# Output weights split once into stored hi and lo tiles, between attention and retention of a hybrid decoder step

## The chip, the cores and the metric

The kernel runs on one core of one Trainium2 chip. The metric is device time in microseconds (us). Engines are named as in the profile: PE multiplies matrices (PEld loads its weights), DVE is the vector engine, ACT the scalar engine, POOL the GpSimd engine, SP the engine that issues most DMAs. Matmul results land in PSUM, other tiles lie in SBUF, and "scratch" tensors lie in DRAM.

## The reference, cut to what matters

1024 prompt tokens and 64 decode tokens (8 sequences of 8) go through one decoder layer; T = 1088 tokens in all. The mixer has two halves, retention and windowed attention, and both are concatenated ahead of one output projection:

```python
    hn = rms_norm(x, norm_mix_gain)
    proj = hn @ w_in
    q_r, k_r, v_r, g_r, q_s, k_s, v_s = jnp.split(proj, cuts, axis=-1)
    ...
    o_r, new_ret = retention(q_r, k_r, v_r, ret_state, chunk)
    o_r = rms_norm(o_r).reshape(b, t, RET_WIDTH) * jax.nn.silu(g_r)
    ...
    o_s = swa_prompt(q_s, k_s, v_s, attn_sinks)       # decode tokens: swa_sample over a cached window
    ...
    h = x + jnp.concatenate([o_r, o_s], axis=-1) @ w_out
    hf = rms_norm(h, norm_ffn_gain)
    h = h + jnp.square(jax.nn.relu(hf @ w_up)) @ w_down
```

`w_out` is 1024 x 1024.

## The kernel before, in words

Every large product is made of three matmuls: each operand is split into a rounded part "hi" (a cast on ACT to `float32r`) and the rest "lo" (a subtraction on DVE or POOL), and `mm3` adds hi x hi, lo x hi and hi x lo.

The stages, in order of time: the projections for attention; attention over the prompt in eight blocks (`swa_block`), with the retention's q, k and gate projections running beside it (`psf`, `psg` are their PSUM tiles, `gst` the gate tiles); attention of the decode tokens; values and retention in blocks of 128 tokens; the output projection, for the first 544 tokens while retention still runs (`out_early`), then for the second 544 (`out_parts`); the squared-ReLU MLP, first up, then down, which takes the time from about 500 us on.

The code is written in program order and a list scheduler sets the order on each engine; that order is fixed in the built program, and each engine works through its own list. SP's list is a queue of DMA issues: one that waits holds up those behind it. A tile pool with `bufs=n` hands out n buffers for a tag in turn; a new tile waits for the last reader of the one that had its buffer.

Names at the place of the change:

- Prompt attention uses tag `s` (three buffers of 4 KB per partition, softmax scores) and tag `pt` (two buffers, transposed probabilities).
- Decode attention uses one more `s` tile, `s8`. Scores are matmuls `sc` in two rounds (the profile's `sc<-smp,q`); DVE turns each round into `s8` (L480, `s<-smp,nsl,sc`), takes maxima (L350 to L355), ACT the exponentials (L358, after loading its table), POOL multiplies by the inverse sums (L365), PE transposes (`pps`), DVE copies (`pt8`), PE multiplies with the values (`po8`), ACT and DVE split the result (`mhs`, `mls`), and SP stores both.
- Only then does SP load the first tiles of retention (`qt8`, `kt8`, L546 and L547), and PE begins retention of the decode tokens with `rsr8` (L633). Value block 1 is tied behind that by an explicit order (`queued`), and value blocks 8 and 0 (`pst`, weights `wv_hi`, `wv_lo`) come ahead of it.
- The output weights: `wo_pair` loads half rows of two weight tiles into `raw` (three buffers), and `wsplit` (L791, L792) makes hi and lo of each on ACT and DVE (tag `wa`, four buffers). Each weight is split for each half of the tokens, so there are 32 splits of 128 x 512. `mix_load(1, ...)` loads the attention rows of the second half of the tokens from DRAM (`mixah`, `mixal`).

The lines that tie the value blocks to decode retention (`next, decode` runs a step of it; `queued` issues behind the last matmul of what came before), and the split:

```python
    value_block(8)
    ins = value_block(0)
    ins = queued(ins, next, decode)
    ins = queued(ins, value_block, 1)
    ins = queued(ins, next, decode)
    ...
    def halve(hi, lo, src, lo_eng):
        nc.scalar.copy(hi, src)                                        # L791
        lo_eng.tensor_tensor(lo, src, hi.bitcast(F32), ALU.subtract)   # L792
```

Of the kernel before, what the change touches and what calls it, by code (L numbers as in the profile page):

```python
# [11 lines left out]
F32 = mybir.dt.float32  # L12
F32R = mybir.dt.float32r
AF = mybir.ActivationFunctionType
ALU = mybir.AluOpType
# [5 lines left out]
P = 128  # L21
# [8 lines left out]
def tok_tile(t):  # L30
    off = 960 if t == 8 else t * 128
    c = min(off // 384, 2)
    return off, c, off - CH[c][0]
# [3 lines left out]
def hymba_layer(ctx: ExitStack, tc: tile.TileContext, a: dict, o: dict):  # L37
    nc = tc.nc
# [10 lines left out]
    scratch = ctx.enter_context(tc.tile_pool(name="scratch", bufs=1, space=DRAM))  # L49

    def slot(i, dt, name):
        return slots.tile([P, 3072], dt, tag=f"s{i}", name=name)
# [13 lines left out]
    def wload(src, kk, name, lo_eng="p", parts=2, after=()):  # L66
        hi = ring.tile([P, 2048], F32R, tag="whi", name=name + "_hi")
        lo = ring.tile([P, 2048], F32R, tag="wlo", name=name + "_lo")
        n = 2048 // parts
        after = list(after)  # L70
        for h in range(2):
            raw = ring.tile([P, 1024], F32, tag="raw", name=f"{name}_raw{h}", bufs=3)
            for q in range(0, 1024, n):
                nc.sync.dma_start(raw[:, q : q + n], src[:, h * 1024 + q : h * 1024 + q + n])
                if after:
                    load_x(*after.pop(0))
            for q in range(0, 1024, n):
                h_, l_ = (v[:, h * 1024 + q : h * 1024 + q + n] for v in (hi, lo))
                r_ = raw[:, q : q + n]
                nc.scalar.copy(h_, r_)  # L80
                eng = nc.vector if lo_eng[(2 * h + q // n) % len(lo_eng)] == "v" else nc.gpsimd
                eng.tensor_tensor(l_, r_, h_.bitcast(F32), ALU.subtract)
        return hi.rearrange("p (k n) -> p k n", k=kk), lo.rearrange("p (k n) -> p k n", k=kk)
# [44 lines left out]
    g_d = scratch.tile([P, 4, T], F32, name="g_d")  # L128
    ms_hi_d = scratch.tile([P, 4, T], F32, name="ms_hi_d")
    ms_lo_d = scratch.tile([P, 4, T], F32, name="ms_lo_d")  # L130
    y_d = scratch.tile([P, 4, 4, 2, Q], F32, name="y_d")
    u_d = [scratch.tile([P, 2, 2, 7, Q], F32, name=f"u_d{g}") for g in range(8)]

# [87 lines left out]
    sp = attn.enter_context(tc.tile_pool(name="swa", bufs=2))  # L221
# [84 lines left out]
    w = wload(a["w_in"][2], 8, "wkv", "v")  # L306
    for t in range(9):
        off, c, r0 = tok_tile(t)
# [14 lines left out]
        pt = psB.tile([P, 512], F32, tag="t2", name="ptk")[:, :128]  # L323
# [112 lines left out]
            )  # L436


    pr = psB.tile([P, 512], F32, tag="t2", name="prq8")
    for t4 in range(4):  # L440
        col_sums(pr[:, t4 : t4 + 1], q8s[:, t4, :], ones[:, 0:1])
# [19 lines left out]
        nc.sync.dma_start(d_, a[s_])  # L461
    nc.sync.dma_start(o["kc"][:, :, 0:120], kc[:, :, 8:128])
    nc.sync.dma_start(o["vc"][0:120], vc[8:128])
    s8 = sp.tile([P, 4, 256], F32, tag="s", name="s8", bufs=3)[:, :, :192]
    for tt in range(2):
        ps = psB.tile([P, 512], F32, tag="t1", name="sc8")
        for t4 in (2 * tt, 2 * tt + 1):
# [18 lines left out]
    for h, n in ((0, 128), (1, 64)):  # L486
        pp = transposed(s8, h * 128, n, "s")
        pt = nt.tile([P, 512], F32, tag="ntmp", name=f"pt8{h}")
# [20 lines left out]
    for blk in range(4):  # L509
        w = wload(a["w_in"][3 + blk], 8, f"wqk{blk}")  # L510
        dst = qr_d if blk < 2 else kr_d
        for j in range(2):
            m = (blk % 2) * 2 + j
# [6 lines left out]
    for blk in range(2):  # L520
        w = wload(a["w_in"][7 + blk], 8, f"wg{blk}")
# [244 lines left out]
    def mix_block(t, mt, gt):  # L766
        off, c, r0 = tok_tile(t)
        d0 = 64 if t == 8 else 0
        pm = psB.tile([P, 512], F32, tag="t2", name="pm")
        for p_ in range(4):  # L770
            nc.tensor.transpose(
                pm[:, p_ * 128 + d0 : p_ * 128 + 128], mt[d0:, p_ * 128 : p_ * 128 + 128], ident[d0:, d0:]
            )
        src = pm.rearrange("p (k n) -> p k n", k=4)[:, :, d0:]
        g_ = gt[:, :, d0:]
        nc.vector.tensor_tensor(g_, src, g_, ALU.mult)
        for s in range(2):
            b0, b1 = max(off + d0, 2 * Q * s), min(off + 128, 2 * Q * s + 2 * Q)
            if b0 < b1:
                hi, lo = (mix[s, "r" + x].rearrange("p k h n -> p k (h n)")[:, :, b0 - 2 * Q * s : b1 - 2 * Q * s] for x in "hl")  # L780
                g1 = gt[:, :, b0 - off : b1 - off]
                nc.scalar.copy(hi, g1)
                nc.gpsimd.tensor_tensor(lo, g1, hi.bitcast(F32), ALU.subtract)


    def pool(name, bufs=1, side=None, space=None):
        kw = {"space": space} if space else {}
        return tc.tile_pool(name=name, bufs=bufs, side=side, reuse_waits="tile", **kw)
# [5 lines that stand above are left out]
    def wsplit(src, tag, name, lo_eng):  # L794
        w = (mid if tag == "wb" else mw).tile([P, 2, 512], F32R, tag=tag, name=name, bufs=4)
        halve(w[:, 0, :], w[:, 1, :], src, lo_eng)
        return w
# [14 lines left out]
    def mix_load(s, pl):  # L812
        for x, d_ in zip("hl", (ms_hi_d, ms_lo_d)):
            t_ = mix[s, "a" + x] = pl.tile([P, 4, 2, Q], F32R, tag="mixa" + x, name=f"mixa{x}{s}")
            nc.sync.dma_start(
                t_.bitcast(F32).rearrange("p k h n -> p k (h n)"), d_[:, :, 2 * Q * s : 2 * Q * s + 2 * Q]
            )

    def wo_pair(s, m, half):

        raw = mw.tile([P, 1024], F32, tag="raw", name=f"wo{half}{s}_{m}_raw", bufs=3)
        c0 = 512 * (half == "a")
        nc.sync.dma_start(
            raw.rearrange("p (m n) -> p m n", m=2), a["w_out"][m : m + 2, :, c0 : c0 + 512].rearrange("m p n -> p m n")
        )
        for i in range(2):
            yield wsplit(raw[:, i * 512 : i * 512 + 512], "wa", f"wo{half}{s}_{m + i}", nc.vector)

    def out_half(s, half, ps, h, w, first, last):
        for k in range(4):  # L830
# [29 lines left out]
    def out_parts(s, ms, half, psum, pss):  # L860

        for m in ms:
            if m % 2 == 0:
                gen = wo_pair(s, m, half)
            w = next(gen)
            for h in range(2):
                if half == "a":
                    pss[m, h] = psum()
                out_half(s, half, pss[m, h], h, w, half == "a", half == "r")
# [74 lines left out]
    qbh, qbl, kh, kl = split_space([ring.tile([P, 1024], F32R, tag="raw", name=f"qk{i}", bufs=3) for i in range(3)])  # L944
    for i, x in enumerate("hl"):
        mix[0, "r" + x] = slot(6 + i, F32R, "mixr" + x)[:, : 8 * Q].rearrange("p (k h n) -> p k h n", k=4, h=2)
    held, mxr, mxrx = {}, None, ExitStack()
    for t in range(5):
        if t == 0:
            for _ in range(2):  # L950
# [4 lines left out]
        if t == 1:  # L955
            hn0x.close()
            mxr = mxrx.enter_context(pool("mxr"))
# [10 lines left out]
    mw = ctx.enter_context(pool("mw", side="right"))  # L968
# [10 lines left out]
    def out_early(m):  # L979

        if m and m % 2 == 0:
            gens["a"], gens["r"] = (wo_pair(0, m, x) for x in "ar")
            ahead.extend(next(gens[x]) for x in "ar")
        wa_, wr_ = ahead
        ahead.clear()
        if m % 2 == 0:
            ahead.extend(next(gens[x]) for x in "ar")
        pss = [early() for h in range(2)]
        for h in range(2):
            out_half(0, "a", pss[h], h, wa_, True, False)  # L990
            out_half(0, "r", pss[h], h, wr_, False, True)
        residual(0, m, pss)()

    gens = {x: wo_pair(0, 0, x) for x in "ar"}
    ahead = [next(gens[x]) for x in "ar"]
    mix_block(4, *held[4])
    for t in (5, 6, 7):
        mt = retention_block(t)
        for m in (2 * t - 10, 2 * t - 9):
            out_early(m)  # L1000
        if t == 6:
            with tc.issue_after(last_load[0].ins):
                mix_load(1, mxA)
        mix_block(t, *mt)
# [218 lines left out]
    for g, (f0, nf) in enumerate(((0, 2), (2, 4), (6, 4), (10, 4), (14, 2))):  # L1223
# [7 lines left out]
        for i in DOWN:  # L1231
# [38 lines left out]
            n = 7 * g - 7 + DOWN.index(i)  # L1270
# [128 lines left out]
```

## Time and profile before

| | |
|---|---|
| median of three runs | 1189.5 us (1188.86 to 1191.59) |
| the profiled execution, whole time | 1188.43 us |
| its span | 1186.7 us |
| PE busy | 1169.6 us |
| DVE busy | 839.1 us |
| ACT busy | 513.8 us |
| POOL busy | 494.2 us |
| granted TensorE clock | 1.00 |

The span runs from the first to the last instruction of the program, and the time of the execution has 1.7 us around it. Busy time is an average over stages: which engine a stage waits for has to be read in that stage. A matmul's row lasts longer than PE is held by it (successive rows overlap), so the pitch of their starts is PE's pace.

### The profile page before, as it was taken

What the parts mean: (1) busy time and instruction counts of PE and PEld (TensorE: products, weight loads), DVE (VectorE), ACT (ScalarE), POOL (GpSimd) and SP (SyncE); (2) the same over time, 40 slices, a digit from 0 to 9 for tenths busy, and PEclk for the clock granted to TensorE, in tenths of its full rate; (3) what the DMA queues carried; (4) which work ended last, traced back from release to release, by engine and by line L of the source; (5) the groups of instructions that cost most, each with busy time, mean ns of one, the idle gap of its engine ahead of it and who ended that gap; (6) DMA issues with size and microseconds to landing.
All of it is one profiled execution on the core that took longest, in us unless ns stands there. A gap on an engine that the chain in (4) does not pass through costs nothing.

```text
span 1186.7 us, 23488 instructions
## 1 busy us (share of the span) xinstructions
PE 1169.6 (99%) x9405; PEld 1123.5 (95%) x9405; DVE 839.1 (71%) x1546; ACT 513.8 (43%) x1055; POOL 494.2 (42%) x393
## 2 busy tenths in 40 slices
PE   8999999999999999999999999999999999999998
PEld 7999988989778899999999999999989999999998
DVE  7556868632257769887766667666788787888676
ACT  8343544553334347644444444444642333333231
POOL 0125333332255542467666666566383142053000
PEclk9999999999999999999999999999999999999999
DMA  7221235333525555343444434444685456443225
GB/s 247 73 62 68 93 102 166 104 115 98 180 74 168 181 183 156 113 156 133 141 151 148 144 130 141 151 148 157 236 290 157 148 169 203 143 155 104 76 59 187
DMA packets 102277, 169.44 MB, mean 143 GB/s; under 512 B 12000, under 2 KB 68256, under 8 KB 101912
## 3 DMA queue, kind: packets, MB, share of 16 engines
q1 hardware_dynamic: 88807, 123.80, 31.5%
q10 hardware_dynamic: 10800, 35.23, 9.3%
q0 software_dynamic: 2560, 8.91, 2.3%
q8 instruction: 74, 1.21, 0.4%
q14 instruction: 36, 0.29, 0.1%
HBM read 114.30 MB, written 53.61 MB: 142 GB/s over the span
## 4 chain that ended last, share of the span: by engine, by line
PE 81%; DVE 6%; DMA 5%; issue 3%; ACT 2%; POOL 2%; SPq 0%; ACTq 0%; DVEq 0%; POOLq 0%
PE psd L176 9%; PE psd L177 9%; PE psd L175 9%; PE psx L175 5%; PE psx L177 5%; PE psx L176 5%; PE psz L175 2%; PE psz L177 2%; PE psz L176 2%; PE pst L175 2%; PE pst L176 2%; PE pst L177 2%; PE psf L175 2%; PE psf L177 2%; PE psf L176 2%
## 5 line engine op out<-in xcount | busy, mean ns | idle before, releaser
L175 PE MATMUL psd<-uh,wd_w 128*128 128x272 f32 x896 | 258.4, 288 | 3.2 <-DVE a L1267 2.4
L176 PE MATMUL psd<-uh,wd_w 128*128 128x272 f32 x896 | 259.3, 289 | 0.0
L177 PE MATMUL psd<-ul,wd_w 128*128 128x272 f32 x896 | 257.9, 288 | 0.7 <-DVE ul L792 0.7
L175 PEld LDWEIGHTS psd<-uh,wd_w 128*128 128x128 f32 x896 | 169.1, 189 | 4.3 <-DVE a L1267 3.4
L177 PEld LDWEIGHTS psd<-ul,wd_w 128*128 128x128 f32 x896 | 168.7, 188 | 0.9 <-DVE ul L792 0.9
L176 PEld LDWEIGHTS psd<-uh,wd_w 128*128 128x128 f32 x896 | 168.4, 188 | 0.0
L1267 DVE TENSOR_TENSOR a<-a,psd 128x272 f32<-128x272 f32 x248 | 101.9, 432 | 48.9 <-PE psd L177 48.8
L792 DVE TENSOR_TENSOR wu_w<-wu_s,wu_w 128x512 fp32r<-128x512 f32 x64 | 61.9, 971 | 49.8 <-ACT wu_w L791 49.2
L791 ACT CAST wd_w<-wd_s 128x512 fp32r<-128x512 f32 x64 | 37.5, 621 | 119.0 <-PE psd L177 107.2
L792 DVE TENSOR_TENSOR ul<-ur,uh 128x1088 fp32r<-128x1088 f32 x56 | 84.0, 1527 | 4.1 <-ACT uh L791 4.1
L1120 DVE SCALAR_TENSOR_TENSOR m<-m,rsf 128x272 f32<-128x272 f32 x96 | 72.9, 760 | 3.2 <-ACT rsf L914 0.5
L175 PE MATMUL psx<-op_1h,wu_w 128*128 128x272 f32 x256 | 74.3, 290 | 0.4 <-ACT m L1136 0.4
L177 PE MATMUL psx<-op_1l,wu_w 128*128 128x272 f32 x256 | 74.1, 289 | 0.0
L175 PE MATMUL psx<-op_0h,wu_w 128*128 128x272 f32 x256 | 74.1, 290 | 0.0
L177 PE MATMUL psx<-op_0l,wu_w 128*128 128x272 f32 x256 | 74.1, 289 | 0.0
L176 PE MATMUL psx<-op_1h,wu_w 128*128 128x272 f32 x256 | 73.7, 288 | 0.0
L176 PE MATMUL psx<-op_0h,wu_w 128*128 128x272 f32 x256 | 73.7, 288 | 0.0
L365 POOL TENSOR_TENSOR sp<-sp,ssp 128x1024 f32<-128x1024 f32 (+1 forms) x16 | 28.6, 1787 | 88.4 <-DVE ssp L364 60.1
L791 ACT CAST uh<-ur 128x1088 fp32r<-128x1088 f32 x56 | 59.7, 1101 | 12.7 <-PE psd L176 9.1
L175 PE MATMUL psf<-hnh,wqk_hi 128*128 128x384 f32 (+1 forms) x192 | 63.5, 331 | 0.2 <-DVE qkst L517 0.2
L177 PE MATMUL psf<-hnl,wqk_hi 128*128 128x384 f32 (+1 forms) x192 | 63.2, 329 | 0.0
L176 PE MATMUL psf<-hnh,wqk_lo 128*128 128x384 f32 (+1 forms) x192 | 62.8, 327 | 0.0
(343 smaller groups left out, 3619.4 us busy)
## 6 DMA issues: line engine op xcount, KB each, us to landing
ur<-u_d SPq DMA_DIRECT2D x53, 544.0 KB, 5.2
u_d<-r4t SPq DMA_DIRECT2D x32, 544.0 KB, 4.6
wu_r<-in_w_up ACTq DMA_DIRECT2D x32, 512.0 KB, 4.4
wd_r<-in_w_down ACTq DMA_DIRECT2D x30, 512.0 KB, 6.5
u_d<-r3t SPq DMA_DIRECT2D x32, 408.0 KB, 2.9
y<-in_xY POOLq DMA_DIRECT2D x16, 272.0 KB, 3.5
y_d<-y POOLq DMA_DIRECT2D x16, 272.0 KB, 3.2
yt<-y_d SPq DMA_DIRECT2D x16, 272.0 KB, 2.9
```

The lines of the kernel that those rows point to most:

```text
L175: nc.tensor.matmul(ps, lh, rh, start=first, stop=False, skip_group_check=more)
L176: nc.tensor.matmul(ps, ll, rh, start=False, stop=False, skip_group_check=more)
L177: return nc.tensor.matmul(ps, lh, rl, start=False, stop=last, skip_group_check=more)
L365: nc.gpsimd.tensor_tensor(s, s, ss.unsqueeze(2).broadcast_to([P, 4, n]), ALU.mult)
L791: nc.scalar.copy(hi, src)
L792: lo_eng.tensor_tensor(lo, src, hi.bitcast(F32), ALU.subtract)
L1120: nc.vector.scalar_tensor_tensor(t_, src, 0.0, rsf[:, s, h, :], ALU.max, ALU.mult)
L1267: added[i] = nc.vector.tensor_tensor(to, to, ps, ALU.add).ins
```

## The change

Between prompt attention and decode attention a new loop loads each of the eight weight tiles whole, splits both halves of it on ACT and DVE, and stores hi and lo side by side in DRAM (`wo_d`) by DMAs that POOL issues. It takes its raw tiles from tag `s` and its split tiles from tag `pt`. `s8` is asked for ahead of the loop. `wo_pair` then loads a split half tile (512 KB) straight into one of seven buffers, four of tag `wa` and three of tag `raw`, with no work on ACT or DVE. The second half's attention rows are loaded one retention block later (`t == 7`).

```diff
+    wo_d = [scratch.tile([P, 2, 1024], F32, name=f"wo_d{m}") for m in range(8)]
...
+    s8 = sp.tile([P, 4, 256], F32, tag="s", name="s8", bufs=3)[:, :, :192]
+    for m in range(8):
+        raw = sp.tile([P, 4, 256], F32, tag="s", name=f"wo_raw{m}", bufs=3).rearrange("p k n -> p (k n)")
+        nc.sync.dma_start(raw, a["w_out"][m])
+        for c in (slice(0, 512), slice(512, 1024)):
+            w = sp.tile([P, 2, 512], F32R, tag="pt", name=f"wo_hl{m}")
+            nc.scalar.copy(w[:, 0, :], raw[:, c])
+            nc.vector.tensor_tensor(w[:, 1, :], raw[:, c], w[:, 0, :].bitcast(F32), ALU.subtract)
+            nc.gpsimd.dma_start(wo_d[m][:, :, c], w.bitcast(F32))
+
     pr = psB.tile([P, 512], F32, tag="t2", name="prq8")
...
-    s8 = sp.tile([P, 4, 256], F32, tag="s", name="s8", bufs=3)[:, :, :192]
...
     def wo_pair(s, m, half):
-        raw = mw.tile([P, 1024], F32, tag="raw", name=f"wo{half}{s}_{m}_raw", bufs=3)
         c0 = 512 * (half == "a")
-        nc.sync.dma_start(
-            raw.rearrange("p (m n) -> p m n", m=2), a["w_out"][m : m + 2, :, c0 : c0 + 512].rearrange("m p n -> p m n")
-        )
         for i in range(2):
-            yield wsplit(raw[:, i * 512 : i * 512 + 512], "wa", f"wo{half}{s}_{m + i}", nc.vector)
+            tag, bufs = ("raw", 3) if len(w_loads) % 7 > 3 else ("wa", 4)
+            w = mw.tile([P, 2, 512], F32R, tag=tag, name=f"wo{half}{s}_{m + i}", bufs=bufs)
+            w_loads.append(nc.sync.dma_start(w.bitcast(F32), wo_d[m + i][:, :, c0 : c0 + 512]))
+            yield w
...
-        if t == 6:
+        if t == 7:
             with tc.issue_after(last_load[0].ins):
                 mix_load(1, mxA)
```

The line numbers of the kernel after are 10 higher from the loop on (L480 becomes L490, L633 becomes L643).

The first place is decode attention on DVE; the rows start where `s8`'s scale is ready. Before:

```order
L453 TENSOR_SCALAR nsl8_2162<-nsl8_2162,nslope_287 128x4 [waits DVE_49]
L480 SCALAR_TENSOR_TENSOR s8_2177<-smp_2171,nsl8_2162,sc8_2178 128x192 [waits DVE_49]
L480 SCALAR_TENSOR_TENSOR s8_2177<-smp_2171,nsl8_2162,sc8_2197 128x192
L526 TENSOR_TENSOR gst_3230<-psg_3205,rsb_177 128x384 [waits DMAHW7_49,PE_49]
L480 SCALAR_TENSOR_TENSOR s8_2177<-smp_2171,nsl8_2162,sc8_2178 128x192 [waits PE_49]
L480 SCALAR_TENSOR_TENSOR s8_2177<-smp_2171,nsl8_2162,sc8_2197 128x192 [waits PE_49]
```

After, the rows that end the same way (`wo_hl5` is the split of weight 5, its two rows the halves a and b; DMASW is a DMA issued by POOL, here the store of the half two earlier):

```order
L447 TENSOR_TENSOR wo_hl4_2179<-wo_raw4_2177,wo_hl4_2179 128x512 [waits DMASW6_49,DMAHW4_49,DVE_49,Activation_49]
L447 TENSOR_TENSOR wo_hl4_2183<-wo_raw4_2177,wo_hl4_2183 128x512 [waits DMASW7_49,Activation_49]
L447 TENSOR_TENSOR wo_hl5_2189<-wo_raw5_2187,wo_hl5_2189 128x512 [waits DMAHW6_49,DMASW0_49,Activation_49]
L447 TENSOR_TENSOR wo_hl5_2193<-wo_raw5_2187,wo_hl5_2193 128x512 [waits DMASW1_49,Activation_49]
L490 SCALAR_TENSOR_TENSOR s8_2136<-smp_2260,nsl8_2251,sc8_2266 128x192 [waits DVE_49]
L490 SCALAR_TENSOR_TENSOR s8_2136<-smp_2260,nsl8_2251,sc8_2285 128x192
L447 TENSOR_TENSOR wo_hl6_2199<-wo_raw6_2197,wo_hl6_2199 128x512 [waits DMAHW1_49,DMASW2_49,Activation_49]
L490 SCALAR_TENSOR_TENSOR s8_2136<-smp_2260,nsl8_2251,sc8_2266 128x192 [waits PE_49]
L490 SCALAR_TENSOR_TENSOR s8_2136<-smp_2260,nsl8_2251,sc8_2285 128x192 [waits PE_49]
```

The score rows moved behind both halves of split 5, with the splits of weights 0 to 4 ahead of them since the scale was ready, and a half of split 6 stands between the two rounds. On ACT the exponentials of decode attention have moved likewise, behind the cast of 7a:

```order
L446 CAST wo_hl6_2203<-wo_raw6_2197 128x512 [waits DMASW3_49,DVE_49]
L446 CAST wo_hl7_2209<-wo_raw7_2207 128x512 [waits DMAHW2_49,DMASW4_49,DVE_49]
L359 ACT_TABLE_LOAD [waits DVE_49]
L359 ACTIVATE s8_2136,sss_2310<-s8_2136,mxs_2304,rq8_2250 128x192 [waits Pool_49]
L359 ACTIVATE s8_2136,sss_2310<-s8_2136,mxs_2304,rq8_2250 128x192 x3
```

Before, gate tiles stood there, and no split. The second place is PE at the start of retention. Before, `rsr8` came straight out of value block 0 (`pst`), and the decode attention's matmuls stood earlier, among the gate and value matmuls:

```order
L177 MATMUL pst_3446<-wv1_lo_3378,hnh0_174 128x512
L633 MATMUL rsr8_3472<-qt8_3361,kt8_3362 64x64 x4
L633 MATMUL rsr8_3479<-qt8_3361,kt8_3362 64x64 x4
L603 MATMUL pkr8_3486<-c_ident_115,kt8_3362 128x128 x4
L175 MATMUL pst_3496<-wv0_hi_3367,hnh0_174 128x512
```

After:

```order
L178 MATMUL pst_3534<-wv1_lo_3466,hnh0_182 128x512
L485 MATMUL sc8_2266<-smp_2260,q8_283 32x128 x4
L485 MATMUL sc8_2266<-k8_298,q8_283 32x64 x4
L485 MATMUL sc8_2285<-smp_2260,q8_283 32x128 x4
L485 MATMUL sc8_2285<-k8_298,q8_283 32x64 x4
L371 MATMUL pps_2319<-c_ident_115,s8_2136 128x128 x4
L371 MATMUL pps_2326<-c_ident_115,s8_2136 64x128 x4
L504 MATMUL po8_2333<-pt81_2331,v8_299 64x256 x2
L507 MATMUL po8_2333<-pt80_2324,smp_2260 64x32 x16
L643 MATMUL rsr8_3560<-qt8_3449,kt8_3450 64x64 x4
L643 MATMUL rsr8_3567<-qt8_3449,kt8_3450 64x64 x4
L613 MATMUL pkr8_3574<-c_ident_115,kt8_3450 128x128 x4
```

The second round of scores, the transposes and the value products of decode attention have moved behind value block 0, next to `rsr8`. The third place is SP's queue at retention blocks 6 and 7. Before, the second half's attention rows stood ahead of `qt7`:

```order
L547 DMA kt7_4705<-kr_d_131 128x4x128
L549 DMA gt6_4475<-g_d_133 128x4x128
L815 DMA mixah1_4692<-ms_hi_d_134 128x4x544
L815 DMA mixal1_4694<-ms_lo_d_135 128x4x544
L546 DMA qt7_4704<-qr_d_130 128x4x128
```

After:

```order
L556 DMA qt6_4551<-qr_d_130 128x4x128
L835 DMA wor0_3_4642<-wo_d3_139 128x2x512
L557 DMA kt7_4773<-kr_d_131 128x4x128
L559 DMA gt6_4555<-g_d_133 128x4x128
L556 DMA qt7_4772<-qr_d_130 128x4x128
L835 DMA woa0_4_4859<-wo_d4_140 128x2x512
L559 DMA gt7_4776<-g_d_133 128x4x128
L825 DMA mixah1_4987<-ms_hi_d_134 128x4x544
```

The rows now come behind `qt7` and `gt7`, and there is a load for each split half weight where one load before fetched a pair.

More of the change, by code (lines that the diff above doesn't have):

```diff
@@ L946, in hymba_layer @@
         mix[0, "r" + x] = slot(6 + i, F32R, "mixr" + x)[:, : 8 * Q].rearrange("p (k h n) -> p k h n", k=4, h=2)
-    held, mxr, mxrx = {}, None, ExitStack()
+    held, mxr, mxrx, w_loads = {}, None, ExitStack(), []
     for t in range(5):
```

## The prediction

> **What bounds the kernel now.** I read the first lines of the page and its chain, then busy time by stretches, then the stretch at the new code row by row. The chain names the engine that ends last:
>
> ```profile
> span 1186.7 us, 23488 instructions
> ...
> PE 1169.6 (99%) x9405; PEld 1123.5 (95%) x9405; DVE 839.1 (71%) x1546; ACT 513.8 (43%) x1055; POOL 494.2 (42%) x393
> ...
> PE 81%; DVE 6%; DMA 5%; issue 3%; ACT 2%; POOL 2%; SPq 0%; ACTq 0%; DVEq 0%; POOLq 0%
> ```
>
> PE is busy 99% of the span, so work of other engines counts only where PE waits for it. By stretches (length; busy us of PE, PEld, DVE, ACT, POOL; clock, DMA share, GB/s):
>
> ```profile
> 285.00:297.00 12.00, 12.00 (x84) 9.61 (x83) 0.92 (x2) 2.74 (x4) 7.18 (x6) 1.00 0.45 118
> ...
> 365.00:390.00 25.00, 23.67 (x249) 21.98 (x248) 21.34 (x44) 10.06 (x17) 13.52 (x11) 1.00 0.61 191
> 390.00:415.00 25.00, 23.62 (x263) 22.02 (x262) 18.39 (x41) 10.35 (x18) 12.92 (x13) 1.00 0.62 201
> ...
> 450.00:480.00 30.00, 30.00 (x285) 29.83 (x284) 28.70 (x72) 21.00 (x48) 7.00 (x9) 1.00 0.52 163
> ```
>
> From 365 to 415 PE pauses a little, and DVE is nearly full at 450 to 480: there the weight splits are removed. At 285 to 297 PE is full and DVE almost empty: near there they are put. What matters is what PE lives on at that place. Rows of the timeline (start, duration, what ended the idle time before), and one of the DMA issues:
>
> ```profile
> 267.04 0.74 DVE L480 SCALAR_TENSOR_TENSOR s<-smp,nsl,sc 128x192 f32<-128x192 f32 x2
> 270.82 0.42 PE L475 MATMUL sc<-smp,q 64*32 64x128 f32 x8
> 272.20 0.95 DVE L350 TENSOR_REDUCE mxs<-s 128x4 f32<-128x768 f32 x1
> 274.15 1.28 ACT L358 ACT_TABLE_LOAD   x1
> 277.58 0.19 ACT L362 ACTIVATE ess<-ess 128x4 f32<-128x4 f32 x1
> 278.35 1.47 POOL L365 TENSOR_TENSOR s<-s,sss 128x768 f32<-128x768 f32 x1 [12.02 <-DVE sss L364]
> 281.93 1.04 PE L370 MATMUL pps<-c_ident,s 128*128 128x128 f32 x8
> 282.57 1.28 DVE L489 COPY pt<-pps 128x512 f32<-128x512 f32 x2 [0.61 <-PE pps L370]
> 287.30 0.65 PE L494 MATMUL po<-pt,v 64*64 64x256 f32 x4
> 287.88 1.12 PE L497 MATMUL po<-pt,smp 128*64 128x32 f32 x32
> 289.05 0.37 ACT L504 CAST mhs<-po 128x256 fp32r<-128x256 f32 x1 [0.89 <-PE po L497]
> 292.18 0.64 SPq L547 DMA_DIRECT2D kt<-kr_d  x1
> 298.49 0.96 PE L633 MATMUL rsr<-qt,kt 64*64 64x64 f32 x16
> ...
> kt<-kr_d SPq DMA_DIRECT2D x9, 256.0 KB, 3.6
> ```
>
> From scores (`sc`) to decode retention (`rsr`) PE needs another engine's answer five times, and gate and value matmuls lie between; it never stops. `rsr` needs `kt`, loaded 2.8 us after `mhs` was cast (289.42 to 292.18) and landing 3.6 later: 6.4 us from `mhs` to the earliest `rsr`.
>
> **The change, part by part.** In the order of the changed program, PE does all gate matmuls and value blocks 8 and 0 first; then second scores, `pps`, `po` and `rsr` follow each other with nothing between, and value block 1 is tied behind `rsr`. The second scores wait for DVE, whose first score rows (L490) stand behind split 5b: `s8` now shares its buffer with raw weight 5. So I follow the chain of splits. Its prices, from the timeline, the tiles' views and the DMA issues (KB each, median us to landing):
>
> ```profile
> 262.87 0.59 ACT L425 CAST mh<-po 128x512 fp32r<-128x512 f32 x1 [1.02 <-PE po L421]
> ...
> L791 ACT CAST woa<-woa_raw x16: 603/620/624, 371.6 to 478.1; 128x512 fp32r<-128x512 f32 x16
> L792 DVE TENSOR_TENSOR woa<-woa_raw,woa x16: 680/692/1065, 373.8 to 478.8; 128x512 fp32r<-128x512 f32 x16
> ...
> u_d<-r4t SPq DMA_DIRECT2D x32, 544.0 KB, 4.6
> ...
> L841 POOL DMA_DIRECT2D y_d<-y x16: 717/726/795, 402.7 to 500.4; - x16
> DMA to landing us min/median/max: 2.6/3.1/7.5
> ...
> wd_r<-in_w_down ACTq DMA_DIRECT2D x30, 512.0 KB, 6.5
> ...
> 273.08 0.49 DVE L526 TENSOR_TENSOR gst<-psg,rsb 128x320 f32<-128x320 f32 x1
> 278.10 0.54 DVE L526 TENSOR_TENSOR gst<-psg,rsb 128x384 f32<-128x384 f32 x1
> 285.80 2.00 ACT L80 CAST wv_hi<-wv_raw 128x1024 fp32r<-128x1024 f32 x2 [3.22 <-PE psg L177]
> 286.92 4.72 POOL L82 TENSOR_TENSOR wv_lo<-wv_raw,wv_hi 128x1024 fp32r<-128x1024 f32 x2 [7.10 <-ACT wv_hi L80]
> ```
>
> A half weight costs ACT 0.62, DVE 0.69 and a 512 KB store issued by POOL (0.73). Before has no such store. Nearest are the 272 KB POOL stores (3.1, the landing row under L841), 544 KB from SP in the same direction (4.6), and 512 KB loads at the crowded end (6.5). I take 4.6, the nearest in size and direction; ends 3.1 and 6.5. There are two split buffers (the old `pt`, free when `po` of the last prompt block is read, about 262.8), so half n waits until half n-2 has landed.
>
> Step by step, in us of the span, 0.1 for a hand-over, "a" and "b" the halves: store 0a issues at 264.2, 0b at 266.0 (behind a memset on POOL), 1a at 270.4 (268.8 landing + 0.62 + 0.69 + hand-overs). 1b's cast stands on ACT behind the gate tile of 273.08 (0.6 earlier now), so 274.5. 2a's subtraction stands on DVE behind the gate tile of 278.10 (about 0.9 earlier now, as score and `pps` matmuls leave its way): 278.6. 2b 280.7, 3a 284.8. 3b: its cast stands behind both `wv_hi` casts on ACT, which wait for PE's last gate matmul (now near 284), and its store behind both `wv_lo` on POOL: 290.3. 4a 291.0, 4b 296.4, 5a 298.4; 5b is subtracted at 302.5. Then L490 twice (0.8), second scores on PE (to 304.0), split 6a, L490 again (305.3), the reduction 0.95, split 6b (its cast waits for 5b's store, 307.1; done 308.6), the maxima (0.6, estimated; 309.2). ACT must cast 7a (6a's store lands 309.2) before table load and exponentials, 3.6 as from 274.15 to 277.77: 313.5. 0.6 to POOL (277.77 to 278.35), POOL 1.47, `pps` 1.04, copies 1.28, `po` 0.65 + 1.12, `mhs` 0.37 and a hand-over: 320.2. Plus 6.4: `rsr` at 326.6 instead of 298.49: **+28.1 us**, all open on PE, which has run out of work at about 295.2 (298.49 less 3.3 of decode matmuls). The same steps with landings of 3.1 give `rsr` at 321.6 (+23.1), with 6.5 at 331.8 (+33.3). Even if stores landed at once, 3b's place behind `wv_lo` and the bare work after it give 313 (+15).
>
> The Trainium skill, "DMA: Bandwidth & Descriptors", section "Anatomy of one DMA — SWDGE (gpsimd) path", fits a GpSimd-issued DMA as 2.0 us and bytes over 436 GB/s; for 512 KB that is an estimate of 3.2 us, and the sum by it would be +23.5 instead of +28.1. For the 272 KB stores it gives 2.6 where the landing row has a median of 3.1, so I keep to the row.
>
> What leaves the output projection: 32 x 0.62 of ACT and 32 x 0.69 of DVE (16 of the 32 splits come back in the new place). They ran beside PE's matmuls except where PE waits. PE's waits from 365 to 540 (total, times, longest), SP's queue, the landing of `qt` in that stretch, and PE's pitch:
>
> ```profile
> PE pm L771 <- DVE mtr L619: 1.3, 1, 1.3
> PE rsr L175 <- ACT qkb L709: 1.2, 1, 1.2
> PE psz L176 <- DVE wu_w L792: 0.9, 1, 0.9
> ...
> 390.64 0.63 SPq L815 DMA_DIRECT2D mixal<-ms_lo_d  x1
> 391.37 0.57 SPq L546 DMA_DIRECT2D qt<-qr_d  x1
> ...
> DMA to landing us min/median/max: 9.2/9.2/9.2
> ...
> 383.28 0.29 PE L175 MATMUL pso<-mixah,woa 128*128 128x272 f32 x1
> 383.41 0.29 PE L176 MATMUL pso<-mixah,woa 128*128 128x272 f32 x1
> ```
>
> These three are PE's longer waits there, 3.4 us (two more are 0.4 and 0.2). The second is the load of `qt` for block 7, which took 9.2 us behind two 1088 KB row loads; the change puts those behind it. The third is DVE late with splits. I take 2.0 of the 3.4: the first wait comes from a late `qt` 6 (before it DVE waits for ACT, ACT for the DMA), and that load now stands behind more weight loads. Loads double from 8 to 16 MB in 32 pieces of 512 KB; each waits for the matmuls of the seventh piece before, 24 x 0.125 us apiece (the starts at 383.28 and 383.41), so some 18 us ahead of need against 4 to 5 us of landing: hidden at full buffers. Without that cover one late piece costs PE up to 5 us. Bounds for this part: a gain of 3.4 and a loss of 5.
>
> Sum on the profiled execution, 1188.4 us (1.7 around its span): +28.1 - 2.0 = 1214.5. The median of the runs is 1189.5, 1.1 above it: **1215.6 us**.
>
> **Rivals.** (1) *Stores land quickly*, near 3.1: +23.1 - 3.4, 1209. For it: the small POOL stores. Against it: twice the bytes, beside 118 GB/s of other traffic. (2) *Stores or reloads slow each other*: 6.5 a store gives +33.3, and no gain later: 1223; with a late weight piece 1228. For it: the 7.5 maximum. Against it: the DMA share is only 0.45 at 285 to 297. (3) *Faster*: decode attention is done before PE runs out. It decides at `rsr` near 298.5; then only the later gain stays, 1186 to 1187.5. For it: DVE and ACT are almost idle at 285 to 297. Against it: ACT's exponentials behind cast 7a and DVE's rows behind 5b are fixed in the order, and not even instant landings reach 298.5. (4) *PE restarts slowly after the pause*. In before PE's clock reads 1.00 in every stretch shown, and its longest pause after 240 us is 1.3 us, so no row here prices it.
>
> The Trainium skill, "TensorE: Matmul & The Clock Gate", section "Part 1: The HAM clock gate", says that an idle window of about 3.4 us halves the clock and another 3.4 us of work restores it. By that rule the restart loses an estimated 1.7 to 3.4 us and the result would be about 1218; no run here shows it so far.
>
> **How the numbers follow.** A change of 0.2% (2.4 us) is about what measurement can tell from none. Chances: the forecast (landings of 4 to 5.5) 0.55; (1) 0.2; (2) 0.15; (4) 0.06; faster or unchanged 0.04, of which (3) has 0.03 and a stall just balanced by gains 0.01. The range must hold 1209 and 1223, and 2 us each way for the hand-overs, which I only estimated: 1206 to 1225; outside stay the 1228 and the faster case.
>
> **What would show it.** After: PE rows with 5 to 12 us idle before the second `sc`, `pps` and `rsr`, and `rsr` starting at 322 to 332; stores of `wo_d` of 4 to 5 us; CASTs of `wo_hl` waiting for DMA; slices at 295 to 325 with PE near empty. The later part is right if `qt` 7 no longer takes 9 us and `psz` no longer waits. I am wrong if `rsr` starts by 305, if PE finds other work in the pause, or if waits on `woa` or `wor` loads appear in the projection.

## Result and the profile after

The kernel after takes 1222.43 us (1220.78 to 1224.44, 4 runs), the one before 1189.18 in the same series: ratio 1.0278, 95% interval 1.0260 to 1.0297, slower. Its profiled execution took 1221.69 us with a span of 1219.9, so the spans differ by 33.2 us.

The head of the page after and the row of TensorE's granted clock in 40 slices:

```profile
span 1219.9 us, 23554 instructions
...
PE 1175.8 (96%) x9405; PEld 1128.8 (93%) x9405; DVE 830.7 (68%) x1530; ACT 504.3 (41%) x1038; POOL 496.3 (41%) x409
...
PEclk9999999998599999999999999999999999999999
```

PE's share fell from 99% to 96%, and one slice shows half the clock. PE's longest waits from 240 to 580 us say where (total, times, longest):

```profile
PE sc L485 <- DVE s L490: 12.1, 1, 12.1
PE pps L371 <- POOL s L366: 9.9, 1, 9.9
PE rsr L643 <- DMA kt<-kr_d: 6.3, 1, 6.3
PE rsr L178 <- DVE qkb L720: 1.7, 1, 1.7
```

The first three are decode attention and its way to decode retention, one behind the other. From the timeline of the kernel after, the same steps (start, duration), first rows of retention block 0 and of the up projection, and two `pst` matmuls early and later in value block 1:

```profile
306.11 0.65 PE L485 MATMUL sc<-smp,q 64*32 64x128 f32 x8 [12.12 <-DVE s L490]
317.50 1.97 PE L371 MATMUL pps<-c_ident,s 128*128 128x128 f32 x8 [9.89 <-POOL s L366]
323.26 0.37 ACT L514 CAST mhs<-po 128x256 fp32r<-128x256 f32 x1 [7.87 <-PE po L507]
325.60 0.64 SPq L557 DMA_DIRECT2D kt<-kr_d  x1
329.55 1.57 PE L643 MATMUL rsr<-qt,kt 64*64 64x64 f32 x16 [6.33 <-DMA kt<-kr_d]
333.23 0.63 PE L176 MATMUL pst<-wv_hi,hnh 128*128 128x512 f32 x1
333.66 0.63 PE L177 MATMUL pst<-wv_hi,hnl 128*128 128x512 f32 x1
337.13 0.39 PE L176 MATMUL pst<-wv_hi,hnh 128*128 128x512 f32 x1
337.36 0.40 PE L177 MATMUL pst<-wv_hi,hnl 128*128 128x512 f32 x1
358.73 0.39 PE L176 MATMUL rsr<-qk,qk 128*128 128x256 f32 x1
530.12 0.28 PE L176 MATMUL psx<-op_0h,wu_w 128*128 128x272 f32 x1
```

And the last two of these places before:

```profile
323.30 0.39 PE L175 MATMUL rsr<-qk,qk 128*128 128x256 f32 x1
496.03 0.29 PE L175 MATMUL psx<-op_0h,wu_w 128*128 128x272 f32 x1
```

Decode retention starts 31.1 us later (329.55 against 298.49), retention block 0 35.4, the up projection 34.1, and the span ends 33.2 later. So 31.1 go up to `rsr`, 4.4 more behind it, and 2.2 come back by the end. The 4.4 are the slow clock: PE runs without a pause from `rsr` to block 0, the same rows as before. Stretches after (PE, PEld, DVE, ACT, POOL busy; clock; DMA share; GB/s):

```profile
297.00:303.00 6.00, 0.00 (x0) 0.00 (x0) 1.39 (x2) 1.82 (x3) 1.38 (x2) 0.59 0.57 202
303.00:306.00 3.00, 0.00 (x0) 0.00 (x0) 1.05 (x3) 1.16 (x2) 0.10 (x1) 0.50 0.36 146
...
333.00:335.00 2.00, 2.00 (x7) 1.52 (x6) 0.00 (x0) 0.93 (x1) 0.47 (x1) 0.50 1.15 324
335.00:337.00 2.00, 2.00 (x9) 1.64 (x8) 0.38 (x1) 1.98 (x4) 0.00 (x0) 0.84 1.17 290
...
343.00:345.00 2.00, 2.00 (x6) 1.54 (x5) 0.00 (x0) 0.00 (x0) 0.00 (x0) 0.50 0.00 0
```

While PE has nothing to do the clock falls to 0.50 and stays there until past 335, some 6 us behind `rsr`; `pst` matmuls start 0.43 us apart at 333 and 0.23 apart at 337. At 343 to 345 the clock is at 0.50 once more although PE is busy throughout. Up to this second fall (the start of `pcr`, 340.34) PE lost 2.8 of the 4.4 us, and 1.6 in it.

The stores of the splits, what the casts waited for (us, times), and the landing of the stores, from the view of the tile `wo_hl`:

```profile
L448 POOL DMA_DIRECT2D wo_d<-wo_hl x16: 678/690/822, 263.7 to 317.4; - x16
...
  DMA wo_d<-wo_hl: 22.9, 9
...
DMA to landing us min/median/max: 3.1/5.2/7.4
```

Casts waited 22.9 us for stores, nine times; a store took 5.2 us in the median, and the last was issued at 317.4. The five stores issued from 305.9 on landed in 3.1 to 3.2 us, the eleven ahead of them in 3.7 to 7.4.

### The profile page after: what moved, and what is told of

Same layout as the page of the kernel before. It is cut to its first block, busy times and chain, and to the rows that moved or that the text cites. A ratio compares the mean times of both kernels' runs of the same rounds, so it can differ in the third digit from the quotient of the medians.

```text
span 1219.9 us, 23554 instructions
## 1 busy us (share of the span) xinstructions
PE 1175.8 (96%) x9405; PEld 1128.8 (93%) x9405; DVE 830.7 (68%) x1530; ACT 504.3 (41%) x1038; POOL 496.3 (41%) x409
## 3 DMA queue, kind: packets, MB, share of 16 engines
q1 hardware_dynamic: 94311, 136.38, 33.3%
## 4 chain that ended last, share of the span: by engine, by line
PE 70%; issue 2%; DMA 1%; DVE 1%; POOL 1%; ACT 1%; SPq 0%; POOLq 0%; DVEq 0%; ACTq 0%
PE psd L177 9%; PE psd L176 9%; PE psd L178 9%; PE psx L176 5%; PE psx L178 5%; PE psx L177 5%; PE psz L176 3%; PE psz L178 3%; PE psz L177 3%; PE pso L176 2%; PE pso L178 2%; PE pso L177 2%; PE psy L176 1%; PE psy L178 1%; PE psy L177 1%
```

## Experiments

Theory A: PE's pause makes the loss, because decode attention stands behind a split chain paced by stores. Rival B: the doubled bytes of the loads in the projection make it. All ratios are against the kernel before, run on the same chip, with 95% intervals.

**The loop alone, and the loads alone.** First the loop added to the kernel before, its result unused:

```diff
     (kernel before)
+    s8 = sp.tile([P, 4, 256], F32, tag="s", ...)      # at its new place
+    for m in range(8): ...                            # the loop, as in the change
```

> The kernel before with the loop of splits and stores alone added, at its new place; the projection still loads raw weights and splits them itself, and nobody reads the stored tiles. Theory A (the loss is PE's pause, made by the split chain ahead of decode attention): the pause is there in full, decode retention (rsr) starts near 329 as in the changed kernel, and without the later gain of some 3 us the time is 1223 to 1227. Rival B (the loss comes from loading twice the bytes in the projection): little is lost here, under 1196.

Measured: 1222.2 us, ratio 1.0287 (1.0260 to 1.0314), a little under the range; `rsr` as expected:

```profile
330.92 1.57 PE L643 MATMUL rsr<-qt,kt 64*64 64x64 f32 x16 [6.76 <-DMA kt<-kr_d]
...
334.00:336.00 2.00, 2.00 (x8) 1.57 (x8) 0.26 (x1) 0.35 (x1) 0.18 (x1) 0.84 1.04 305
```

The second row is a stretch: here the clock is back at about 334.5, 3.6 us behind `rsr`, and it doesn't fall again. From `rsr` to block 0 this run loses 1.6 us to the clock, where the kernel after loses 4.4; that offsets most of the later gain, which it doesn't have.

The other half, the changed kernel with one weight split and loaded 32 times:

```diff
-    for m in range(8):
+    for m in range(1):
...
-            ... wo_d[m + i][:, :, c0 : c0 + 512]))
+            ... wo_d[0][:, :, c0 : c0 + 512]))
```

> The changed kernel with the loop cut to weight 0 (two halves instead of sixteen), and all 32 loads of the projection taken from that one stored weight, so the output is of wrong weights; bytes and number of the loads stay. Theory A: no pause, rsr within 1 us of 298.5, and the projection's gain alone is left: 1185 to 1188. Rival B: the loads still cost, 1205 or more.

Measured: 1186.85 us, 0.9988 (0.9976 to 1.0001); span 1184.6 against 1186.7, `rsr` at 298.61. So the loop makes the loss, and the projection's loads cost nothing: B falls. What the projection gains is some 2 us by the medians and the spans; the interval reaches 1.0001, so it can't be told from nothing by the times alone.

**What in the loop holds PE.** `s8` with a buffer of its own:

```diff
-    s8 = sp.tile([P, 4, 256], F32, tag="s", name="s8", bufs=3)[:, :, :192]
+    s8 = sp.tile([P, 4, 192], F32, tag="s8", name="s8", bufs=1)
```

> The changed kernel with one edit: s8 has a buffer of its own instead of one that raw weights 2 and 5 use. If the shared buffer is what puts decode attention behind the splits (theory A1), second scores, pps and po go back among gate and value matmuls and rsr starts at 298 to 302; splits 4b to 7b are then still ahead of retention's rows on DVE and ACT and end near 312, so PE stops some 8 us at ror behind value block 1, 2 to 3 more for a slow clock, and with the later gain of 3 the time is 1195 to 1200. If the pace of the stores decides whatever the buffers (A2): rsr at 315 or later, 1212 or more.

Measured: 1208.0 us, 1.0164 (1.0135 to 1.0192): between the two, both missed. The shared buffer is worth 14 of the 33 us. Second scores and `pps` are back among the gate matmuls (`pps` waits 0.6 instead of 9.9), yet `rsr` comes at 307.7. SP's queue and PE say why:

```profile
295.98 0.52 SPq L376 DMA_DIRECT2D ms_lo_d<-mls  x1
299.93 0.33 SPq L443 DMA_DIRECT2D wo_raw<-in_w_out  x1
300.37 0.59 SPq L556 DMA_DIRECT2D qt<-qr_d  x1
301.00 0.63 SPq L557 DMA_DIRECT2D kt<-kr_d  x1
...
307.71 1.57 PE L643 MATMUL rsr<-qt,kt 64*64 64x64 f32 x16 [5.23 <-DMA kt<-kr_d]
319.78 2.00 PE L664 MATMUL ror<-tabS,rptr 64*64 64x64 f32 x16 [3.02 <-DVE rptr L648]
```

A raw weight's load waits in SP's queue for its buffer, and `qt` and `kt` stand behind it until 300.4: `kt` is issued 5.0 us behind the store of `mls`. Then `ror` waits for `rptr`, which stands on DVE behind the last split, ended at 319.2.

The loop written behind decode attention:

```diff
-    s8 = ... and the loop, ahead of decode attention
...
     mix_store(mh, ml, 1024, 64)
+    for m in range(8): ...          # the loop; s8 where it was before
```

> The changed kernel with the loop written behind decode attention, and s8 asked for where it was before. Theory A: decode attention goes first, rsr at 298 to 302, and what is left of the splits holds retention's first rows on DVE and ACT until some 312 to 316: 1196 to 1203. Rival A2 (16 MB of stores and loads at this place cost the same wherever they are written): 1212 or more.

Measured: 1218.6 us, 1.0247 (1.0220 to 1.0273): A's range missed by over 15 us. The rival's number came true (it counted 16 MB; the loop moves 12, 8 of stores and 4 of loads). Decode attention is out of the way (`po` at 290.1), but PE waits 16.3 us for `kt`:

```profile
300.41 7.37 SPq L512 DMA_DIRECT2D wo_raw<-in_w_out  x2
307.90 0.59 SPq L557 DMA_DIRECT2D qt<-qr_d  x1
308.54 1.84 SPq L558 DMA_DIRECT2D kt<-kr_d  x1
```

I had counted only DVE and ACT behind the splits. The chain, being later, has two loads ahead of `qt` in SP's queue, the second waiting 7 us for its buffer: here SP's queue carries most of the pause, and `kt` lands in 7.7 us. So much the same loss has another bearer; that the bytes alone set it, as the rival had it, isn't shown.

**What paces the chain.** The loop alone, with stores of an eighth of the bytes:

```diff
-            nc.gpsimd.dma_start(wo_d[m][:, :, c], w.bitcast(F32))
+            nc.gpsimd.dma_start(wo_d[m][:, :, c][:, :, :64], w[:, :, :64].bitcast(F32))
```

> As the run with the loop alone (the projection splits for itself, nobody reads the stored tiles), but each store writes the first 64 of 512 columns, 64 KB instead of 512. If the landing of the stores paces the splits (theory A), rsr comes at 314 to 320 instead of 330.9, near the 313 that the prediction gave for stores that land at once, and the time is 1203 to 1211. If the order on ACT, DVE and POOL sets the pace and not the stores, rsr stays beyond 326 and the time at 1217 or more.

Measured: 1212.0 us, 1.0186 (1.0170 to 1.0202), and `rsr` as expected (time 1 us over the range). Stores land in 3.1 us (median; 2.0 least) instead of 5.3:

```profile
317.64 1.57 PE L643 MATMUL rsr<-qt,kt 64*64 64x64 f32 x16 [6.25 <-DMA kt<-kr_d]
...
wo_d<-wo_hl POOLq DMA_DIRECT2D x16, 64.0 KB, 3.1
```

So the landing of the stores is the greater part of the pace: the casts wait 14.9 us for stores, and 24.1 with the full bytes. 2.2 us less of landing bring `rsr` 13.3 us forward, but these 6 us for each us are not the price of landing alone. The list scheduler built another order: nine casts of the loop stand on ACT ahead of `wv_hi`, and seven in the run with the full bytes. The DMA engines are quieter, too. At block 0 only 10.6 of the 13.3 us are left, as the clock falls a second time here (last section).

Raw loads moved out of SP's queue, on top of `s8`'s own buffer:

```diff
-        nc.sync.dma_start(raw, a["w_out"][m])
+        nc.gpsimd.dma_start(raw, a["w_out"][m])
```

> The changed kernel with a buffer of its own for s8, as before, and the loads of the raw weights issued by POOL instead of SP, so that they no longer hold qt and kt in SP's queue. Both theories: rsr at 299 to 302 instead of 307.7. If the end of the split chain ahead of retention's rows on DVE decides (theory A3), ror still waits until some 318 and the time stays at 1203 to 1209; if SP's queue was the cause of what was left (rival), ror comes by 308 and the time is 1193 to 1199.

Measured: 1203.3 us, 1.0122 (1.0103 to 1.0140), against 1208.0 with the same buffers. The time is as A3 said, the rest is not. `kt` is now issued 1.9 us behind the store of `mls` (299.49 to 301.38) instead of 5.0, so the queue did hold it before. But `rsr` stays at 307.08, since `po` is later (296.1 instead of 291.2). Its operand `pt` stands on DVE behind a split that took 3.91 us:

```profile
288.78 4.90 POOL L82 TENSOR_TENSOR wv_lo<-wv_raw,wv_hi 128x1024 fp32r<-128x1024 f32 x2
...
290.33 3.91 DVE L447 TENSOR_TENSOR wo_hl<-wo_raw,wo_hl 128x512 fp32r<-128x512 f32 x1 [2.58 <-ACT wo_hl L446]
```

A split takes 0.69 us elsewhere. This one began while POOL made `wv_lo`, and it ended at 294.24, 0.56 us behind it. The longest split of the kernel after does the same: 2.41 us, ended at 291.41, `wv_lo` at 290.85. So in these runs DVE's subtraction stood still while POOL subtracted.

The chain ends 3.5 us earlier, `rptr` starts at 315.75 and `ror` at 316.33 without waiting, 9.3 us behind `rsr`; that is what value block 1 takes there at a slow clock (9.7 with the short stores, 7.0 before). So the 3.0 that `ror` waited for the end of the chain are what was won. What is left is more than the late `rsr`: 8.6 us there, 10.9 at `ror` and 15.9 at block 0, as on the way `pcr` waits 1.6 us for POOL and the clock falls again (0.52 from 323 to 326).

Lo in place, so that twice as many halves are under way:

```diff
+        w = sp.tile([P, 2, 512], F32R, tag="pt", ...).rearrange("p i n -> p (i n)")   # hi of a whole weight
         for c in (slice(0, 512), slice(512, 1024)):
+            nc.scalar.copy(w[:, c], raw[:, c])
+            nc.vector.tensor_tensor(raw[:, c].bitcast(F32R), raw[:, c], w[:, c].bitcast(F32), ALU.subtract)
+        nc.gpsimd.dma_start(wo_d[m][:, 0, :], w.bitcast(F32))
+        nc.gpsimd.dma_start(wo_d[m][:, 1, :], raw)
```

> The changed kernel with a buffer of its own for s8, and lo written in place over the raw weight, so that a split buffer holds hi of a whole weight and twice as many halves are under way; hi and lo are stored apart, with the same bytes in all. If two split buffers make the chain slow (theory A), it ends near 302 to 306 instead of 319.5, ror waits 0 to 3 us, and the time is 1186 to 1194. If the DMA engines are full at this place (rival), the chain ends beyond 312 and the time is 1198 or more.

Measured: 1199.4 us, 1.0091 (1.0070 to 1.0113). The chain ends at 303.3, as A said, and DVE no longer holds `ror`; the time is 5 us over A's range. `kt` is issued 8.6 us later than before (300.79 against 292.18), as `mhs` stands on ACT behind casts that wait for a raw weight, and it lands in 8.0 us instead of 3.6, with the DMA engines full:

```profile
296.38 1.14 ACT L446 CAST wo_hl<-wo_raw 128x512 fp32r<-128x512 f32 x2 [5.20 <-DMA wo_raw<-in_w_out]
...
297.00:310.00 13.00, 2.71 (x22) 2.13 (x21) 2.92 (x5) 2.51 (x5) 4.56 (x8) 0.76 1.01 342
...
308.90 1.57 PE L644 MATMUL rsr<-qt,kt 64*64 64x64 f32 x16 [10.29 <-DMA kt<-kr_d]
```

Both theories had a part: two buffers slow the chain, and with more the DMA share reaches 1.01. In none of these orders do the 8 MB of stores and 4 MB of loads fit ahead of decode retention unseen.

**Another place for the loop.** Four quarter pieces of a weight behind each block of prompt attention:

```diff
-    done_swa = [swa_block(c) for c in range(NB)]
+    for c in range(NB):
+        done_swa.append(swa_block(c))
+        wo_split(c)      # 4 x: load 128 KB by POOL, cast, subtract, store 256 KB by POOL; one raw, one split buffer
```

> The loop taken apart: four pieces of 256 columns of one weight behind each block of prompt attention in the code, in buffers of their own (one raw, one split), loads and stores issued by POOL; s8 where it was before; the projection as in the changed kernel. If the loss is only the place of the loop (theory A), rsr keeps within 2 us of 298.5 and the projection's gain remains: 1185 to 1189. If casts that wait for DMAs hold up prompt attention on ACT (rival), its po matmuls end some us later than 262 and the time is 1191 to 1205.

Measured: 1223.1 us, 1.0294 (1.0272 to 1.0316): the rival, and worse than it said: prompt attention's `po` matmuls end at 299.5 instead of 262. Pieces were drawn to the very start of the kernel (first cast at 5.9 us), and there steps of attention stand on DVE behind subtractions that wait for casts and loads. A row of DVE, and PE's longest waits:

```profile
73.44 0.42 DVE L438 TENSOR_TENSOR wo_hl<-wo_raw,wo_hl 128x256 fp32r<-128x256 f32 x1 [11.85 <-ACT wo_hl L437]
...
PE ptk L325 <- DVE kn L320: 11.5, 1, 11.5
PE scp L400 <- DVE sp L402: 9.3, 6, 3.1
```

**The later gain.** The rows of the second half alone, on the kernel before:

```diff
-        if t == 6:
+        if t == 7:
```

> The kernel before with the one edit that the second half's attention rows are loaded at t == 7 instead of 6. Theory A (the prediction's): the wait of rsr for qkb behind the late qt 7 goes, some 1.2 us, and nothing else changes: a span 1.0 to 1.4 us shorter than before. Rival (the later gain comes from the splits that leave DVE and ACT alone): no change, within 0.3 us.

Measured: 1194.05 us, 1.0050 (1.0038 to 1.0062): slower by 5 us, against both. The late load only changed hands. PE waits 3.9 us for the residual sum, which stands on DVE behind the split of a raw weight (`wor_raw`) that lands 9.1 us after its issue, behind the two row loads, and restarts at a low clock (0.86 from 400 to 425):

```profile
400.37 0.63 SPq L815 DMA_DIRECT2D mixah<-ms_hi_d  x1
401.05 0.62 SPq L815 DMA_DIRECT2D mixal<-ms_lo_d  x1
403.82 0.37 SPq L823 DMA_DIRECT2D wor_raw<-in_w_out  x1
...
412.99 0.62 ACT L791 CAST wor<-wor_raw 128x512 fp32r<-128x512 f32 x1 [4.14 <-DMA wor_raw<-in_w_out]
...
PE pso L175 <- DVE y L839: 3.9, 1, 3.9
```

The loads alone, with the rows where they were before:

```diff
     (one weight, loaded 32 times, as above)
-        if t == 7:
+        if t == 6:
```

> As the run with the loop cut to weight 0 and all loads from that one stored weight (output of wrong weights), but the second half's rows loaded at t == 6 as before. Theory A: the wait for the late qt 7 is back, so some 1.2 us of that run's gain of 2.3 go, and the wait of psz for wu_w stays away: 1187.5 to 1188.5. Rival (split removal is the whole gain): as that run, 1186 to 1187.

Measured: 1186.4 us, 0.9988 (0.9974 to 1.0002), span 1183.4: the rival's number, though the two theories lie 1 us apart and the interval is wider. The waits bear it out: `rsr` waits 0.7 us for `qkb` here and 1.7 with the rows at `t == 7`, so the later rows bring no gain, and `psz` waits in neither. With loads instead of splits the rows may stand in either place; what is gained comes from the splits which left.

A version meant to beat both, which stores the first half's splits as they are made:

```diff
             w = wsplit(raw[:, i * 512 : i * 512 + 512], "wa", ...)          # first half of the tokens, as before
+            nc.gpsimd.dma_start(wo_d[m + i][:, :, c0 : c0 + 512], w.bitcast(F32))
...
+            w_loads.append(nc.sync.dma_start(w.bitcast(F32), wo_d[m + i][:, :, c0 : c0 + 512]))   # second half
```

> No loop: the output projection of the first half of the tokens splits the weights as before and POOL stores each split half, 512 KB, as it is made; the second half loads the stored tiles and splits nothing; rows at t == 7. Theory A: no pause, and the gains of the rows and of the missing splits in the second half remain: 1186.5 to 1188.5, the best version with the right result. Rival (stores keep the four split buffers longer, and the projection waits for splits): 1190 to 1198, with waits on woa or wor.

> The version that stores the splits of the first half, with the rows loaded at t == 6 as before. If what cost 13 us there was mostly the raw weight load that now lands late behind the two 1088 KB row loads (as in the run with the rows alone, 5 us), this is 1187 to 1192; if the 512 KB stores themselves slow the stage (buffers held, crowded DMA), 1194 to 1202.

Measured: 1202.9 us, 1.0110 (1.0096 to 1.0125) with the rows at `t == 7`, and 1195.9, 1.0062 (1.0042 to 1.0082) at 6: so both theories had a part, some 7 us for the stores and 6 to 7 more for the rows beside raw loads (5 in the run with the rows alone). With rows at 7 the last `wor_raw` ahead of `mtr` landed 12.6 us after its issue and PE waited 8.0 us:

```profile
PE pm L772 <- DVE mtr L620: 9.8, 2, 8.0
```

No version that computes the reference was faster than the one before.

## Why the prediction was right

The forecast was 1215.6, in 1206 to 1225; it came out at 1222.4, 6.8 higher. In order of its steps:

- *The pause, its place and its bearers*: right. Second scores behind split 5b, exponentials behind 7a, `rsr` last, PE empty between: the waits on `sc`, `pps` and `rsr` are those foreseen, and the loop alone gives the whole loss.
- *`rsr` at 326.6 (+28.1)*: measured 329.55 (+31.1; the run began 0.8 us ahead of the one before, so 31.9). The landing was put at 4.6 and was 5.2. Between the prediction's own ends (23.1 at 3.1, 33.3 at 6.5) that is worth about 1.6; most of the rest is the slow clock ahead of `rsr`, below. One small term was missing: split 3b, beside POOL's `wv_lo`, took 2.41 us instead of 0.69 and its store went out 0.85 us behind `wv_lo`. The Trainium skill, "DMA: Bandwidth & Descriptors", section "Anatomy of one DMA — SWDGE (gpsimd) path", gave an estimate of 3.2 for these 512 KB: here it is the least (3.1), and the median is 5.2. For the 64 KB stores its fit makes an estimate of 2.2, and again the least (2.0) is near and the median (3.1) is not.
- *The price of a us of landing*: 3 us of `rsr` for each us in the working (23.1 to 33.3 over 3.4). The 0.6 us that the landing really was longer fit it. The short stores gave 6, with another order and quieter DMA engines, and came 4 us ahead of the prediction's own 321.6 for landings of 3.1; so the price stays open. The floor of 313 for stores that land at once is not contradicted: 317.6 at 3.1.
- *PE's own steps at full speed*: this term failed. `pps` took 1.97 instead of 1.04 and `rsr` 1.57 instead of 0.96, at a clock of 0.50. This was rival (4), given 0.06 as no row of before could price it. It cost 4.4 us behind `rsr`, and some 2 ahead of it (0.9 in `pps`, the rest in `po`), and the sum had nothing for it.
- The Trainium skill, "TensorE: Matmul & The Clock Gate", section "Part 1: The HAM clock gate", has the clock halved by an idle window of about 3.4 us and restored by a busy one. The trace agrees with the halving. The clock came back 3.6 us behind `rsr` in the run with the loop alone, some 6.0 in the kernel after and 6.4 with the short stores, so not at a fixed 3.4. The estimate of 1.7 to 3.4 us from that rule is near what the restart cost: 1.6 us in the run with the loop alone, 2.3 with raw loads by POOL and 2.8 in the kernel after. The other 1.6 of the 4.4 are the second fall, which that estimate doesn't hold.
- *The later gain of 2.0*: size right as far as it can be told (2.2 by the end of the span; 2.1 and 3.3 in the spans of the two runs with loads alone, whose times can't be told from before), cause partly wrong. I credited 1.2 to the rows that moved behind `qt` 7. The runs show that the edit gains nothing with loads and costs 5 us with splits; in the kernel after, another load is late: one `qt` of that stretch lands in 10.2 us, and `rsr` waits 1.7 for `qkb`. `psz`'s wait for `wu_w` is gone, as foreseen.
- *The doubled loads hidden*: right; no wait on `woa` or `wor`, and the loads alone cost nothing.

The 6.8 us over the forecast are the slow clock's 6 (4.4 and some 2) and the longer landing's 1.6, less the 0.8 of the earlier start. That the range held them is in part luck: its upper end was set by rival (2), stores of 6.5 us and no later gain, and neither came true; a slow restart was in no term of the sum.

## What to carry over

A loop of load, split and store with two buffers is a serial chain, and everything that stands behind one of its links, in any queue or through a shared buffer, takes over its pace: count the chain's end against the next stage's first rows on DVE, ACT and SP. Taking one holder away (the buffer, the place, the queue) won a part, 14 us at most, and handed the rest to the next, until the DMA engines themselves were full. Such an edit also gives the list scheduler another order, so look at the order before you read a price from it. Before moving a large load later, ask which load is queued next behind it; and price a pause of PE with a restart at half clock (1.6 to 2.8 us here behind pauses of 6 to 7 us, and once more if the clock falls again).

## What the hardware showed unexpectedly

The second fall of the clock came with PE busy. In the kernel after, from 340.34 PE ran `pcr`, 16 matmuls that each stream 32 columns, and then full `pst` matmuls at half clock (0.50 at 343 to 345):

```profile
340.34 1.97 PE L672 MATMUL pcr<-tabS,s0v 128*128 128x32 f32 x16
342.47 0.61 PE L177 MATMUL pst<-wv_hi,hnl 128*128 128x512 f32 x1
...
346.11 0.40 PE L177 MATMUL pst<-wv_hi,hnl 128*128 128x512 f32 x1
```

It cost 1.6 of the 4.4 us. The run with the short stores shows it too: `pcr` begins at 328.39 without a pause, and behind it PE is full at a low clock:

```profile
330.00:334.00 4.00, 4.00 (x14) 3.19 (x14) 0.00 (x0) 0.00 (x0) 0.00 (x0) 0.57 0.02 4
```

The same sequence kept its clock before, with lo in place (1.00 from 318 to 327) and in the run with the loop alone, where block 0 starts as late as `ror` does (34.1 us both). So the sequence alone doesn't decide. That its small matmuls count as little activity is a guess that fits the rows; no run tested it.
